# Two shared allocations for the small tiles of a two-layer decoder kernel

## The chip, the cores and the metric

One core of a Trainium2 chip runs the whole program. The metric is device time in microseconds (us) of one execution: the median over the runs of one kernel. Times inside an execution come from one profiled execution of the kernel before.

## The reference

Two layers of a decoder with a model width of 1024 over 256 tokens, all in float32. Layer 0 attends by blocks (at 256 tokens there is one block, so this is causal attention), layer 1 takes the weighted difference of two softmax maps. A SwiGLU FFN of width 2816 follows each. Shift, scale and gate come from a conditioning vector.

```python
c_act = jax.nn.silu(c)
for i in range(DEPTH):
    mod = (c_act @ ada_w[i] + ada_b[i])[:, None, :]
    sh_a, sc_a, g_a, sh_f, sc_f, g_f = jnp.split(mod, 6, axis=-1)
    h = rms_norm(x, norm_g[i, 0]) * (1.0 + sc_a) + sh_a
    y = moba_attention(...) if i % 2 == 0 else diff_attention(...)
    x = x + g_a * rms_norm(y, norm_g[i, 1])
    h = rms_norm(x, norm_g[i, 2]) * (1.0 + sc_f) + sh_f
    x = x + g_f * rms_norm(swiglu(h, ffn_w_in[i], ffn_w_out[i]), norm_g[i, 3])
```

## The kernel before

**Split products.** Every large weight is loaded as float32 in pieces of 128 x 1024 elements into one of eight `raw` buffers (`wpair`, line 497 on). ScalarE writes its rounded high part (line 503), VectorE the rest (line 504), both into one of nine `ring` buffers of 8 KB per partition. A matmul of a weight is then three passes (`mm`, line 506 on): high by high, high by low, low by high. In `mm` (line 512) the stationary operand is a 128 x 128 block of the activation and the moving operand is 512 columns of the ring buffer:

```python
a = h[:, 1 if q == 2 else 0, k]
for p, (b, s) in zip(ps, W):
    nc.tensor.matmul(p[:, :n], a, b[:, 1 if q == 1 else 0, s], start=first and q == 0, stop=last and q == 2)
```

In `mmT` (line 526) it is the other way round: the stationary operand is a block of the ring buffer, and the moving operand is 256 columns of `hh`, the activation of both token tiles.

**Where activations lie.** `hh` holds the split activation that enters QKV, the output projection (`po`) and the first FFN product (`pg`, `pu`, and `pgu` for the last, narrow chunk). The FFN's middle activation `a` goes into four buffers that attention used for q and k: chunk number even into `qT0` (token tile 0) and `qT1` (token tile 1), odd into `kT0` and `kT1`. The second FFN product (`f2`, psum `pf`) has `a` as its stationary operand and a ring buffer `s_u` as its moving one.

**Stages of one execution.** The first conditioning products and the first QKV run to about 60 us, attention and output projection of layer 0 to about 150 us, its FFN to about 325 us, attention of layer 1 to about 450 us, its FFN to the end.

**Order.** Every operation is recorded first; `Schedule.run` then sets one order from a table of priorities and from modelled costs, and gives each buffer a slot of its class. After that the tiles are made in the order in which they are first used, one tag per slot:

```python
for o in order:
    for b in o.bufs:
        if b.cls in ("h0", "h1"):
            b.t = hh[:, int(b.cls[1])]
        elif b.cls and b.t is None:
            b.t = pools.get(b.cls, sb).tile(list(b.shape), b.dt, name=b.name, tag=f"{b.cls}_{b.slot}")
    o.fn()
```

**Small tiles.** `keep` makes tiles that live through the whole program; some are 128 x 1 to 128 x 8 elements (`ones1`, `mh`, `cact`, the `scsh` vectors and others). `sm` makes the vectors of one to four elements of the norms and softmaxes (`ss`, `ms`, `y`, `mx`, `su`, `r`, `so`), in 24 slots. Each small tile and each of the 24 slots is an allocation of its own, which takes a multiple of 32 bytes in every partition, and they are mixed with the large tiles in the order of first use. So a large tile begins 0 or 32 bytes after a multiple of 64.

Of the kernel before, what the change touches and what calls it, by code (L numbers as in the profile page):

```python
# [12 lines left out]
F = mybir.dt.float32  # L13
# [219 lines left out]
def trunk_kernel(ctx: ExitStack, tc: tile.TileContext, x, c, rel_bias, ada_w, ada_b, norm_g, moba_w_qkv, moba_w_o,  # L233
# [4 lines left out]
    const = ctx.enter_context(tc.tile_pool(name="const", bufs=1))  # L238
    sb = ctx.enter_context(tc.tile_pool(name="sb", bufs=1))
# [4 lines left out]
    slots = dict(a=4, bc=4, raw=8, ring=9, z=2, acc=2, s2=8, qT0=1, qT1=1, kT0=1, kT1=1, PT0=2, PT1=2,  # L244
                 v0=1, v1=1, h0=1, h1=1, gate=2, sm=24)
    S_ = Schedule(slots)
    op = S_.op

    def keep(name, shape, dt=F):
        return Buf(name, t=const.tile(list(shape), dt, name=name))  # L250

    def sm(name, w=1):
        return Buf(name, "sm", [128, w])
# [8 lines left out]


    xt = [keep(f"x{t}", [128, D]) for t in range(T)]
    ident = keep("ident", [128, 128])
    ones = keep("ones", [128, 128], R)
    ones1 = keep("ones1", [128, 1])
    mh = keep("mh", [128, 4])
# [616 lines left out]

    order = S_.best()
    pools = dict.fromkeys(("a", "bc"), psum)
    for o in order:
        for b in o.bufs:
            if b.cls in ("h0", "h1"):  # L890
                b.t = hh[:, int(b.cls[1])]
            elif b.cls and b.t is None:
                b.t = pools.get(b.cls, sb).tile(list(b.shape), b.dt, name=b.name, tag=f"{b.cls}_{b.slot}")
        o.fn()
# [102 lines left out]
```

## Time and profile before

| | |
|---|---|
| median of 3 runs | 645.5 us (643.41 to 646.35) |
| the profiled execution's own time | 644.03 us |
| its span, first to last instruction | 642.1 us |
| TensorE busy | 630.3 us (98% of the span) |
| VectorE busy | 474.2 us (74%) |
| ScalarE busy | 366.7 us (57%) |
| share of TensorE in the chain that ended last | 82% |

The span is the part of the profiled execution that the trace covers; some 1.9 us of its own time lie around it. "Busy" adds up the durations of an engine's instructions, where overlapping matmuls count once. The chain is followed back from the last instruction to what released each step; its pieces add up to the span, so a piece of it is time that counts. Granted clock is TensorE's: 1.00 is 2.4 GHz, 0.50 is 1.2 GHz.

### The profile page before, as it was taken

The numbers are of one execution on the slowest core, as the hardware profiler recorded it, in microseconds if no ns is written. First come the engines' busy times: TensorE is split into PE (matmuls) and PEld (weight loads), VectorE is DVE, ScalarE is ACT, GpSimd is POOL, SyncE is SP. The second block draws the span as 40 slices with busy tenths as digits, with TensorE's granted clock in tenths as the row PEclk, the third lists the DMA queues.
The fourth block names the chain that finished last, engine by engine and source line by source line (L and its number), as shares of the span: only waits on it lengthen the run. The fifth ranks groups of instructions, "written<-read, shape, count | busy, mean of one in ns | idle before, by whom it ended". The sixth has DMA issues, their size and how long they took to land.

```text
span 642.1 us, 8916 instructions
## 1 busy us (share of the span) xinstructions
PE 630.3 (98%) x3216; PEld 524.7 (82%) x3216; DVE 474.2 (74%) x603; ACT 366.7 (57%) x616; POOL 31.1 (5%) x66
## 2 busy tenths in 40 slices
PE   8999989999999999999999999999999999999996
PEld 7899978887888888888887997888888888888884
DVE  2798689987788797646599999999546566744453
ACT  4567779378463634444396787949744453543342
POOL 1000000040000000000021000111100000000001
PEclk9799999999999999999999999999999999999999
DMA  9999999998999987657858988455467868645301
GB/s 306 360 335 333 320 332 362 362 308 271 331 306 379 312 304 261 197 167 235 279 194 295 358 284 284 134 174 183 147 219 231 266 220 265 203 141 165 114 1 65
DMA packets 72503, 160.60 MB, mean 250 GB/s; under 512 B 5506, under 2 KB 22531, under 8 KB 72459
## 3 DMA queue, kind: packets, MB, share of 16 engines
q1 hardware_dynamic: 72267, 159.96, 74.2%
q8 instruction: 25, 0.41, 0.3%
q14 instruction: 19, 0.16, 0.1%
q10 hardware_dynamic: 192, 0.08, 0.0%
HBM read 158.69 MB, written 1.33 MB: 249 GB/s over the span
## 4 chain that ended last, share of the span: by engine, by line
PE 82%; DMA 5%; DVE 5%; ACT 3%; issue 2%; POOL 1%; DVEq 0%; POOLq 0%; SPq 0%; ACTq 0%
PE pf L512 18%; PE pu L512 17%; PE pg L512 17%; PE po L512 5%; PE pv L512 5%; DMA bias<-toep 4%; PE pq L526 4%; PE pgu L512 3%; PE pq L512 2%; PE warm L307 2%; PE po L696 2%; PE pa L299 1%; DVE a L379 1%; ACT s_q L503 1%; DVE s_q L504 1%
## 5 line engine op out<-in xcount | busy, mean ns | idle before, releaser
L512 PE MATMUL pg<-s_i,hh 128*128 128x512 f32 x480 | 190.6, 397 | 0.1
L512 PE MATMUL pu<-s_i,hh 128*128 128x512 f32 x480 | 189.6, 395 | 0.0
L504 DVE TENSOR_TENSOR s_i<-w_i,s_i 128x1024 fp32r<-128x1024 f32 (+1 forms) x96 | 107.5, 1133 | 60.3 <-ACT s_i L503 60.0
L503 ACT ACTIVATE s_i<-w_i 128x1024 fp32r<-128x1024 f32 (+1 forms) x96 | 94.1, 987 | 89.7 <-PE pu L512 45.1
L512 PE MATMUL pf<-s_u,a 128*128 128x512 f32 x528 | 140.5, 397 | 0.0
L512 PEld LDWEIGHTS pf<-s_u,a 128*128 128x128 f32 x528 | 97.8, 188 | 22.3 <-ACT a L841 0.4
L512 PEld LDWEIGHTS pg<-s_i,hh 128*128 128x128 f32 x480 | 90.1, 188 | 21.9 <-ACT hh L548 0.5
L512 PEld LDWEIGHTS pu<-s_i,hh 128*128 128x128 f32 x480 | 90.2, 188 | 21.2
L379 DVE SCALAR_TENSOR_TENSOR acc<-aw,cact,acc 128x1024 f32<-128x1024 f32 x70 | 89.1, 1278 | 3.1 <-DMA aw<-in_ada_w_dram 2.5
L503 ACT ACTIVATE s_u<-w_u 128x1024 fp32r<-128x1024 f32 x44 | 46.5, 1059 | 58.5 <-PE pu L512 36.7
L504 DVE TENSOR_TENSOR s_u<-w_u,s_u 128x1024 fp32r<-128x1024 f32 x44 | 53.5, 1223 | 30.9 <-ACT s_u L503 30.5
L526 PE MATMUL pq<-hh,s_q 128*128 128x256 f32 x480 | 61.5, 285 | 0.7 <-ACT hh L548 0.7
L526 PEld LDWEIGHTS pq<-hh,s_q 128*128 128x128 f32 x480 | 59.3, 190 | 2.8 <-issue 0.9
L512 PE MATMUL po<-s_o,hh 128*128 128x512 f32 x192 | 50.3, 403 | 0.0
L512 PEld LDWEIGHTS po<-s_o,hh 128*128 128x128 f32 x192 | 35.0, 188 | 7.2
L504 DVE TENSOR_TENSOR s_q<-w_q,s_q 128x1024 fp32r<-128x1024 f32 x32 | 38.3, 1219 | 2.2 <-ACT s_q L503 2.2
L503 ACT ACTIVATE s_q<-w_q 128x1024 fp32r<-128x1024 f32 x32 | 32.9, 1056 | 6.7 <-DMA w_q<-in_moba_w_qkv_dram 4.1
L491 POOL TENSOR_SCALAR ms<-ss 128x1 f32<-128x1 f32 x16 | 9.4, 588 | 510.3 <-ACT z L577 502.0
L512 PE MATMUL pgu<-s_i,hh 128*128 128x512 f32 x96 | 26.5, 398 | 0.0
L512 PE MATMUL pv<-s_q0v,hh 128*128 128x512 f32 x96 | 24.9, 401 | 0.9 <-ACT s_q0v L503 0.9
L658 ACT ACTIVATE sx<-sx,mx 128x256 f32<-128x256 f32 (+1 forms) x48 | 21.3, 445 | 6.9 <-DVE mx L656 6.8
L512 PE MATMUL pv<-s_q1v,hh 128*128 128x512 f32 x96 | 24.7, 403 | 0.0
(142 smaller groups left out, 724.9 us busy)
## 6 DMA issues: line engine op xcount, KB each, us to landing
aw<-in_ada_w_dram SPq DMA_DIRECT2D x80, 512.0 KB
w_i<-in_ffn_w_in_dram SPq DMA_DIRECT2D x80, 512.0 KB
w_u<-in_ffn_w_out_dram SPq DMA_DIRECT2D x44, 512.0 KB
aw<-in_ada_w_dram SPq DMA_DIRECT2D x32, 256.0 KB
w_q<-in_moba_w_qkv_dram SPq DMA_DIRECT2D x16, 512.0 KB
w_q<-in_diff_w_qkv_dram SPq DMA_DIRECT2D x16, 512.0 KB
w_q0v<-in_moba_w_qkv_dram SPq DMA_DIRECT2D x8, 512.0 KB
w_o<-in_moba_w_o_dram SPq DMA_DIRECT2D x8, 512.0 KB
```

The lines of the kernel that those rows point to most:

```text
L299: nc.tensor.transpose(dst[:, o:o + n], a, ident[:n, :n])
L307: nc.tensor.matmul(warm.t[:].rearrange("p (a b) -> p a b", a=4), ones.t[:], ones.t[:, None, :].to_broadcast([128, 4, 128]), start=True, st ...
L379: op("DVE", tt(n) + 0.065, lambda: nc.vector.scalar_tensor_tensor(a.t, w(), cact[:, kc:kc + 1], a.t, op0=OP.mult, op1=OP.add), r=[cact, w. ...
L491: op("POOL", 0.16, lambda: nc.gpsimd.tensor_scalar(ms.t, m0.t[:], 1.0 / n, EPS, op0=OP.mult, op1=OP.add), r=[m0], w=[ms])
L503: op("ACT", ac(2 * n), lambda: nc.scalar.activation(b[:, 0], w.t[:], AF.Copy), r=[w], w=[(b, K(0))], name="hi" + name)
L504: op("DVE", tt(2 * n), lambda: nc.vector.tensor_sub(b[:, 1], w.t[:], b[:, 0].bitcast(F)), r=[w, (b, K(0))], w=[(b, K(1))], name="lo" + name)
L512: nc.tensor.matmul(p[:, :n], a, b[:, 1 if q == 1 else 0, s], start=first and q == 0, stop=last and q == 2)
L526: nc.tensor.matmul(p[:, j * 256:j * 256 + 256].rearrange("p (t q) -> p t q", t=T), b[:, 1 if q == 1 else 0, s, c + j * 128:c + j * 128 + 1 ...
L658: op("ACT", ac(nk, 2), lambda i=i, sx=sx, mx=mx, su=su: nc.scalar.activation(sx[:, i], sx[:, i], AF.Exp, bias=mx[:, i:i + 1], accum_out=su ...
L696: nc.tensor.matmul(p[:, i * 128:i * 128 + 128], a, b, start=kt == 0, stop=kt == t)
```

## The change

Small tiles no longer have allocations of their own. One allocation `small` (128 x 112 elements) holds what `keep` used to make with at most eight elements in a row, at steps of 16 or 32 bytes; one allocation `smt` (128 x 192) holds the 24 slots of `sm`, at steps of 32 bytes.

```diff
+    small = const.tile([128, 112], F, name="small")
+    small_at = [0]
+
     def keep(name, shape, dt=F):
-        return Buf(name, t=const.tile(list(shape), dt, name=name))
+        if len(shape) > 2 or shape[1] > 8:
+            return Buf(name, t=const.tile(list(shape), dt, name=name))
+        o = small_at[0]
+        small_at[0] += 4 if shape[1] <= 4 else 8
+        assert small_at[0] <= 112
+        return Buf(name, t=small[:shape[0], o:o + shape[1]])
 ...
+    smt = sb.tile([128, 8 * slots["sm"]], F, name="smt")
     for o in order:
         for b in o.bufs:
             if b.cls in ("h0", "h1"):
                 b.t = hh[:, int(b.cls[1])]
+            elif b.cls == "sm":
+                b.t = smt[:, 8 * b.slot:8 * b.slot + b.shape[1]]
             elif b.cls and b.t is None:
```

Every engine executes the same operations on tiles of the same shapes, in the same order. On TensorE, VectorE, GpSimd and SyncE each instruction also waits for the same semaphore values. On ScalarE 13 of 546 instructions wait at another place: a wait for GpSimd on a reused small slot stands one or two instructions later, and five instructions that only wait are gone.

What differs is where tiles begin. All large tiles have sizes that are multiples of 128 bytes, so without small ones between them they all begin at the same offset from a multiple of 128. Read from the two built programs, in bytes within a partition:

| tile | begins before, modulo 128 | begins now, modulo 128 |
|---|---|---|
| `hh` | 0 | 64 |
| `qT0`, `kT1` (hold `a`) | 96 | 64 |
| `kT0` (holds `a`) | 32 | 64 |
| `qT1` (holds `a`) | 0 | 64 |
| `ring` buffers (`s_q`, `s_i`, `s_u`, `s_o`) | 96 (eight of nine), 32 (one) | 64 |
| `raw` buffers | 96 or 32 (seven of eight), 0 (one) | 64 |
| `ones`, `ident`, `x` | 0 | 64 |

So every large tile now begins at a multiple of 64.

## Rows read from the trace of the kernel before

**Rows 1.** The page: span, and busy time, share and instructions of TensorE.

```profile
span 642.1 us, 8916 instructions
PE 630.3 (98%) x3216; PEld 524.7 (82%) x3216; DVE 474.2 (74%) x603; ACT 366.7 (57%) x616; POOL 31.1 (5%) x66
```

**Rows 2.** Busy time by stage: window, its length, each engine, granted clock, DMA.

```profile
core 0: us, PE busy (x) PEld busy (x) DVE busy (x) ACT busy (x) POOL busy (x), PEclk, DMA share, GB/s
0.00:60.00 60.00, 57.19 (x383) 52.91 (x384) 43.15 (x81) 34.06 (x61) 2.82 (x16) 0.91 1.01 336
60.00:150.00 90.00, 87.76 (x502) 74.89 (x501) 78.42 (x95) 65.81 (x134) 9.40 (x12) 1.00 0.99 333
150.00:325.00 175.00, 175.00 (x778) 141.53 (x777) 125.96 (x134) 85.56 (x104) 0.93 (x3) 1.00 0.79 270
325.00:450.00 125.00, 124.39 (x734) 105.71 (x733) 121.25 (x185) 97.06 (x209) 14.36 (x26) 1.00 0.73 245
450.00:642.10 192.10, 185.99 (x826) 149.66 (x824) 105.38 (x112) 84.25 (x111) 3.60 (x9) 1.00 0.52 169
```

**Rows 3.** The chain by line, windows 60:150, 150:325, 325:450 and 449:643.

```profile
by line: DMA bias<-toep 30.7%; PE po L512 13.6%; PE pv L512 13.0%; PE po L696 5.9%; issue 5.8%; ACT z L577 3.1%; PE ppt L299 2.7%; DVE x L590 2.5%; POOL ms L493 2.1%; ACT hm L543 2.1%; DVE z L587 2.1%; POOL y L494 1.9%; DVE z L557 1.5%; DVE
...
by line: PE pf L512 30.9%; PE pu L512 29.6%; PE pg L512 29.4%; PE pgu L512 6.4%; PE pa L299 2.6%; PE pgr L482 0.3%; PE pgr L483 0.3%; ACT sg L837 0.2%; issue 0.2%; PE pgc L401 0.2%; ACT z L577 0.1%
...
by line: PE pq L526 18.5%; PE pv L512 18.3%; PE po L512 18.0%; PE pq L512 10.8%; ACT s_q L503 5.2%; PE ps L648 4.8%; PE po L696 4.3%; ACT z L577 2.3%; PE pg L512 2.2%; ACT hm L543 2.1%; PE ppt L299 2.1%; PE pu L512 2.1%; POOL ms L491 1.6%; 
...
by line: PE pf L512 31.6%; PE pg L512 27.8%; PE pu L512 27.8%; PE pgu L512 5.8%; PE pa L299 2.5%; PE ph L299 0.5%; DVE x L590 0.4%; DVEq L993 0.3%; ACT z L577 0.3%; POOLq L993 0.3%; PE pgr L482 0.2%; PE pgr L483 0.2%; issue 0.1%; POOL ms L4
```

**Rows 4.** Chain pieces (start us, us, what): stationary `hh`, first and last of eight, then 23.

```profile
515.85 0.23 PE pu L512
...
517.48 0.24 PE pg L512
...
116.68 5.37 PE po L512 x23
```

**Rows 5.** Chain pieces of `pf`: `a` in `qT0`, `kT1`, `kT0`, `qT1`; last, `qT0`.

```profile
623.26 2.04 PE pf L512 x9
...
530.21 1.81 PE pf L512 x8
...
318.10 2.80 PE pf L512 x12
...
629.25 3.26 PE pf L512 x14
...
192.89 0.93 PE pf L512 x4
```

**Rows 6.** Busy time, columns as in rows 2, around three of those pieces.

```profile
530.20:532.00 1.80, 1.80 (x10) 1.36 (x8) 0.37 (x1) 1.06 (x1) 0.00 (x0) 1.00 0.71 216
623.30:625.30 2.00, 2.00 (x10) 1.66 (x9) 0.00 (x0) 0.00 (x0) 0.00 (x0) 1.00 0.00 0
629.30:632.50 3.20, 3.20 (x15) 2.59 (x14) 2.77 (x5) 0.84 (x4) 0.93 (x3) 1.00 0.00 0
```

**Rows 7.** Chain pieces just before 623.26, and the 512-column warm-up matmuls.

```profile
622.33 0.23 PE pgu L512
622.56 0.70 PE pf L512 x3
...
7.98 0.93 PE warm L307 x4
```

**Rows 8.** Chain pieces of line 526 (256 columns), and the transposes of `a` by line.

```profile
372.19 4.89 PE pq L526 x40
...
L299 PE MATMUL pa<-ident,sg 128*128 128x128 f32 x88 | 13.5, 272 | 0.0
```

**Rows 9.** VectorE and ScalarE on `w_u`: count, then ns minimum/median/maximum.

```profile
L503 ACT ACTIVATE s_u<-w_u x44: 1041/1060/1104, 161.3 to 616.8; 128x1024 fp32r<-128x1024 f32 x44
L504 DVE TENSOR_TENSOR s_u<-w_u,s_u x44: 1215/1224/1227, 162.4 to 617.9; 128x1024 fp32r<-128x1024 f32 x44
```

## The prediction

> **What bounds the kernel now.** I read the page first: TensorE is busy 630.3 of 642.1 us [rows 1]. A busy engine can still be one that waits in small pieces, so the busy times by stage come next [rows 2]. In the two FFN stages (150 to 325 us, and 450 us to the end) TensorE is busy all the time but for the last few us, the clock is at its upper level (1.00, 2.4 GHz), and DMA, VectorE and ScalarE have room. In the first 150 us the DMA share is about 1, and from 325 to 450 us VectorE is busy for 121.25 of 125 us. The chain of waits says the same [rows 3]: in the FFNs the matmuls of 512 columns (`pf`, `pu`, `pg`, `pgu`) are 96.3% and 93.0% of the chain, that is 168.5 us of 175 and 179 us of 193. So the time hangs on how fast matmuls of 512 columns follow each other, and the question is whether the place of a tile in memory changes that pace.
>
> The duration of a matmul in the trace doesn't tell the pace, since matmuls overlap; the length of a chain piece divided by its count does. I looked for pieces whose tiles I can name, and set them beside the table of offsets in the section on the change. Where the stationary operand is `hh` (offset 0) and the moving one a ring buffer (offset 96, modulo 128), eight pieces begin 1.63 us from first to last, seven steps of 233 ns; a run of 23 in the output projection takes 5.37 us, 233.5 ns each [rows 4]. In the second FFN product the stationary operand changes its buffer [rows 5]. With `a` in `qT0` (96) and a ring buffer at 96, nine take 2.04 us: 226.7 ns each. With `a` in `kT1` (also 96) eight take 1.81 us: 226.3 ns. With `a` in `kT0` (32) against 96, twelve take 2.80 us: 233.3 ns. With `a` in `qT1` (0) against 96, fourteen take 3.26 us: 232.9 ns. The last row is the one ring buffer at 32 with `a` in `qT0` at 96: four take 0.93 us, 232.5 ns. The reading is: **equal offsets modulo 128 give 226.7 ns, unequal ones 233.3 ns**, 6.6 ns or 2.8% more. Other traffic doesn't explain it [rows 6]: the piece at 226.3 ns (530 us) stands beside a DMA share of 0.71 and a busy ScalarE, the one at 232.9 ns (629 us) beside no DMA at all.
>
> The short step doesn't begin at once. The four pieces ahead of the nine at 226.7 ns take 0.93 us, 232.5 ns each, the first of them with `hh`, three already at equal offsets [rows 7]. So after a break of the pattern some four or five matmuls still go at about 232 ns.
>
> **The change part by part.** *Small tiles into two allocations:* the same operations with the same shapes; ScalarE loses five instructions that only wait, and 13 of its waits stand a little later. ScalarE is busy about half of each FFN stage [rows 2], so I cost this at nothing; it would count only if ScalarE became late for TensorE.
>
> *Large tiles move, for VectorE and ScalarE:* the 44 splits of `w_u` read all eight `raw` buffers and write the ring buffers, at all the mixed offsets of today, and VectorE's durations lie between 1215 and 1227 ns, ScalarE's between 1041 and 1104 [rows 9]. With medians of 1224 and 1060 this bounds a common offset to under 2% in either direction, on engines that aren't the bound in the FFNs: nothing.
>
> *Large tiles move, for the transfers:* no row tells one buffer's transfers from another's. The chain of 60 to 150 us holds 27.6 us of transfers (30.7% of 90) [rows 3]; half a per cent either way would be 0.1 us, and I take nothing. The Trainium skill (DMA: Bandwidth & Descriptors, "How a descriptor splits into AXI transactions") speaks against the change here: a piece that doesn't start at a multiple of 256 bytes costs one transaction more. One `raw` buffer of eight starts at such a multiple before and none does now, so by that page one load in eight of 2 KB pieces would need nine transactions in place of eight; as an estimate that is some 1.5% of the 90 us with a DMA share of 0.99, or plus 1.4 us. No row here shows it.
>
> *Large tiles move, for TensorE:* every pair of operands is now at equal offsets (64 and 64). The sum, piece by piece:
> - FFNs, 347.5 us of chain in 512-column matmuls. `pf` is 30.9% of 175 and 31.6% of 193, together 115 us; half of its matmuls have equal offsets already (`qT0` and `kT1` against the eight ring buffers). So 290 us go at unequal offsets, and 2.8% of that is 8.2 us. The other 57 us mix 226.7 and 232 ns and may gain 0 to 1 us as their neighbours stop breaking the pattern; I take 0.5.
> - Breaks remain: 88 transposes of `a` [rows 8] in groups of two to four, so some 22 to 44 breaks of five matmuls at 232 instead of 226.7 ns, 27 ns each: 0.6 to 1.2 us to give back. I take 0.9.
> - 325 to 450 us: `po`, `pv`, `pq` of line 512, `pg` and `pu` are 51.4% of the chain, 64 us; 2.8% is 1.8 us. VectorE has only 3.75 us of room in this stage [rows 2], so I count half, 0.9.
> - 60 to 150 us: `po` and `pv` are 26.6% of 90 us; 2.8% is 0.7 us, beside a DMA share of 0.99. I count 0.2.
> - Line 526 (ring buffer stationary, `hh` moving, 256 columns) takes 122 ns in a run of 40 [rows 8], always at unequal offsets. What equal offsets give there no row shows: between nothing and the same 6.6 ns each, which on 23 us of chain (18.5% of 125) is up to 1.3 us. I take nothing, since its stage is the one short of VectorE.
>
> 8.2 + 0.5 - 0.9 + 0.9 + 0.2 = 8.9 us. Against the profiled execution's 644.03 us this is 635.1; that execution is 0.2% under the median of the runs, 645.5, from which the same sum gives 636.6. I put the forecast between them, at **635.8 us**. With every uncertain term at its best (8.2 + 1.0 - 0.6 + 1.8 + 0.7 + 1.3) the gain is 12.4 us, from 644.03 a time of 631.6. If the next limit came up, it would be VectorE between 325 and 450 us; in the FFNs it has over 49 us of room.
>
> **The rivals.** *The offset is not the cause.* The short steps could come from something else that the two places share, for instance that no matmul there waits. For it: the warm-up matmuls have `ones` as both operands, so equal offsets, and four of them take 0.93 us, 232.5 ns [rows 7]; they stand so soon after a break that they may not have settled, and they read 128 columns four times over. Against it: seven places [rows 4, 5], busy and quiet, sort by offset alone. Then the time stays at 644 to 645.5 us. The Trainium skill (TensorE: Matmul & The Clock Gate, Part 2, "Step-by-step") stands on this side: "Loading the next tile's weights doesn't steal SBUF read bandwidth from the running matmul", so by it the two operands' places shouldn't matter to each other. The rows of 226.7 and 233.3 ns differ in just that.
>
> *The gain is partial.* The pattern is broken too often to settle, so that matmuls stay near 231.5 ns. Then 290 us gain 0.8%, 2.3 us, with the rest some 3 us: 641 us. The run of nine at 623 us settled within five, which speaks against it.
>
> *Slower.* All tiles at one offset could bring the weight load and the stream into each other's way for good. The place would be every 512-column matmul, 1490 of them on the FFN chain (347.5 us at 233 ns). From 235.5 ns on, 2.2 ns more each, that is 3.3 us and counts; at 237 ns it would be 649 us. For it: 64 against 64 occurs nowhere in this trace, and only pairs at 96 show the short step. Against it: no run at equal offsets is above 233 ns.
>
> *The change doesn't do what it says.* The offsets in the built program are all 64, so only the rivals above remain.
>
> **How the numbers follow.** The forecast (632 to 639 us) gets 0.66, the partial gain 0.12, no effect 0.13, slower 0.09. Half a per cent, 3.2 us, is about what a measurement of this kernel can tell from no change. The partial gain lies at that bound and is halved: faster 0.66 + 0.06 = 0.72, same 0.06 + 0.13 = 0.19, slower 0.09. The range goes from 631, where all uncertain terms are at their best, to 643, which takes in the partial gain and leaves out most of no effect and all of slower, about 0.2 together.
>
> **What would show it.** In the new trace, runs of `pg` and `pu` in the FFNs should step by about 227 ns, with four or five at 232 after each group of transposes; the two FFN stages should be 8 us shorter together. `pf` from `qT1` and `kT0` should be as fast as from `qT0`. VectorE's 1224 ns and ScalarE's 1060 ns should stand. The prediction is wrong in its mechanism if `pg` and `pu` still step by 233 ns, and wrong in its sum if they step by 227 and the stage between 325 and 450 us, or the first 150 us, gets longer.

## The result, and the profile after

| kernel | median us (lowest to highest) | ratio to before, 95% interval |
|---|---|---|
| before | 644.45 (642.31 to 646.35) | |
| changed | 636.17 (634.17 to 636.36) | 0.9865 [0.9825, 0.9905] |
| changed, measured again beside the kernel before | 635.19 (633.97 to 636.89) | 0.9866 [0.9844, 0.9887] |

The changed kernel is 1.35% faster, 8.3 us between the medians; the forecast was 635.8 us. Its profiled execution has a span of 634.5 us, 7.6 us under the 642.1 of before. The page of the changed kernel, span and busy times, answers to [rows 1]:

```profile
span 634.5 us, 8911 instructions
PE 621.5 (98%) x3216; PEld 525.8 (83%) x3216; DVE 473.8 (75%) x603; ACT 367.1 (58%) x616; POOL 31.9 (5%) x66
```

TensorE's busy time fell by 8.8 us with the same 3216 instructions; VectorE, ScalarE and GpSimd stand within 0.8 us of before. Busy time by stage in the changed kernel, columns as in [rows 2]; the borders are set where its own stages end:

```profile
core 0: us, PE busy (x) PEld busy (x) DVE busy (x) ACT busy (x) POOL busy (x), PEclk, DMA share, GB/s
0.00:60.00 60.00, 57.21 (x379) 53.45 (x379) 42.78 (x81) 33.65 (x61) 2.83 (x16) 0.89 1.02 335
60.00:150.00 90.00, 87.12 (x505) 75.34 (x504) 78.41 (x94) 65.85 (x135) 9.42 (x12) 1.00 0.99 333
150.00:322.00 172.00, 172.00 (x780) 141.91 (x779) 126.37 (x135) 86.31 (x107) 0.93 (x3) 1.00 0.80 275
322.00:442.00 120.00, 119.04 (x716) 102.18 (x715) 116.75 (x180) 94.06 (x202) 14.07 (x24) 1.00 0.72 245
442.00:634.50 192.50, 186.16 (x844) 152.92 (x842) 109.48 (x117) 87.28 (x116) 4.61 (x11) 0.99 0.54 176
```

The stages look as in [rows 2]: TensorE fills the first FFN stage, and VectorE is busy for 97% of the second attention stage, as before. Fixed windows hide where time went, so I take landmarks: the first matmul of each product. The tile view gives count, ns minimum/median/maximum, then the first and last start in us. First the kernel before:

```profile
L512 PE MATMUL pv<-s_q0v,hh x96: 388/396/498, 75.1 to 109.7; 128*128 128x512 f32 x96
L512 PE MATMUL pg<-s_i,hh x240: 388/394/503, 139.5 to 301.2; 128*128 128x512 f32 x120
L512 PE MATMUL pq<-s_q,hh x96: 388/394/484, 332.5 to 362.3; 128*128 128x512 f32 x96
L512 PE MATMUL pg<-s_i,hh x240: 388/394/477, 442.5 to 612.9; 128*128 128x512 f32 x120
L512 PE MATMUL pf<-s_u,a x528: 387/394/482, 171.4 to 635.6; 128*128 128x512 f32 x176
```

and the changed kernel, in which line 512 has become 521:

```profile
L521 PE MATMUL pv<-s_q0v,hh x96: 387/389/500, 75.8 to 110.2; 128*128 128x512 f32 x96
L521 PE MATMUL pg<-s_i,hh x240: 387/389/499, 139.8 to 298.4; 128*128 128x512 f32 x120
L521 PE MATMUL pq<-s_q,hh x96: 387/389/477, 329.2 to 358.9; 128*128 128x512 f32 x96
L521 PE MATMUL pg<-s_i,hh x240: 387/389/486, 438.8 to 605.7; 128*128 128x512 f32 x120
L521 PE MATMUL pf<-s_u,a x528: 387/389/486, 171.2 to 628.0; 128*128 128x512 f32 x176
```

The start of one landmark taken from the start of the next gives a stage:

| stage | before, us | changed, us | difference | predicted |
|---|---|---|---|---|
| start to first `pv` | 75.1 | 75.8 | +0.7 | 0 |
| first `pv` to first `pg` (attention, layer 0) | 64.4 | 64.0 | -0.4 | -0.2 |
| first `pg` to first `pq` (FFN, layer 0, and what leads to `pq`) | 193.0 | 189.4 | -3.6 | |
| first `pq` to next `pg` (attention, layer 1) | 110.0 | 109.6 | -0.4 | -0.9 |
| that `pg` to last `pf` (FFN, layer 1) | 193.1 | 189.2 | -3.9 | |
| the two FFN stages | 386.1 | 378.6 | -7.5 | -7.8 |
| last `pf` to end of span | 6.5 | 6.5 | 0 | 0 |

The median duration of one of these matmuls went from 394 to 389 ns. As they overlap, the pace (the step from one start to the next) is read from the chain of waits: the length of a piece divided by its count. Pieces of the changed kernel's chain (start us, us, what), in the order of [rows 4], [rows 5] and [rows 8]:

```profile
504.84 0.23 PE pu L521
...
506.43 0.23 PE pg L521
...
115.56 7.27 PE po L521 x32
...
615.20 3.64 PE pf L521 x16
...
621.11 7.30 PE pf L521 x32
...
368.80 4.98 PE pq L535 x40
```

From 504.84 to 506.43 there are seven steps, so 227 ns each, against 233 in [rows 4]; 32 steps of `po` in 7.27 us make 227.2 against 233.5 before. `pf` with `a` in `qT0` (615.20) takes 227.5 ns and with `a` in `qT1` (621.11) 228.1, both with some slower steps at their start that follow transposes; `qT1` stood at 232.9 in [rows 5].

### The profile page after: what moved, and what is told of

The parts are those of the page before. It is cut to its first block, busy times and chain, and to the rows that moved or that the text cites. A ratio compares the mean times of both kernels' runs of the same rounds, so it can differ in the third digit from the quotient of the medians.

```text
span 634.5 us, 8911 instructions
## 1 busy us (share of the span) xinstructions
PE 621.5 (98%) x3216; PEld 525.8 (83%) x3216; DVE 473.8 (75%) x603; ACT 367.1 (58%) x616; POOL 31.9 (5%) x66
## 3 DMA queue, kind: packets, MB, share of 16 engines
q1 hardware_dynamic: 72267, 159.96, 74.8%
## 4 chain that ended last, share of the span: by engine, by line
PE 81%; ACT 5%; DMA 4%; DVE 4%; issue 2%; POOL 2%; POOLq 0%; DVEq 0%; SPq 0%; ACTq 0%
PE pf L521 18%; PE pg L521 16%; PE pu L521 16%; PE po L521 5%; PE pv L521 5%; PE pq L535 5%; DMA bias<-toep 4%; PE pgu L521 3%; PE pq L521 2%; PE warm L316 2%; PE po L705 2%; ACT s_q L512 2%; PE pa L308 1%; ACT z L586 1%; ACT hm L552 1%
## 5 line engine op out<-in xcount | busy, mean ns | idle before, releaser
L521 PE MATMUL pg<-s_i,hh 128*128 128x512 f32 x480 | 188.2, 392 | 0.1
L521 PE MATMUL pu<-s_i,hh 128*128 128x512 f32 x480 | 187.0, 390 | 0.0
L521 PE MATMUL pf<-s_u,a 128*128 128x512 f32 x528 | 138.5, 393 | 0.0
L388 DVE SCALAR_TENSOR_TENSOR acc<-aw,small,acc 128x1024 f32<-128x1024 f32 x70 | 89.1, 1277 | 3.6 <-DMA aw<-in_ada_w_dram 2.9
L512 ACT ACTIVATE s_u<-w_u 128x1024 fp32r<-128x1024 f32 x44 | 46.6, 1060 | 57.0 <-PE pu L521 30.9
L535 PE MATMUL pq<-hh,s_q 128*128 128x256 f32 x480 | 62.6, 288 | 0.7 <-ACT hh L557 0.7
L500 POOL TENSOR_SCALAR smt<-smt 128x1 f32<-128x1 f32 (+1 forms) x20 | 10.5, 526 | 581.6 <-ACT z L586 495.2
L667 ACT ACTIVATE sx<-sx,smt 128x256 f32<-128x256 f32 (+1 forms) x48 | 21.3, 446 | 6.3 <-DVE smt L665 6.1
```

The costliest lines, as they stand in the source:

```text
L388: op("DVE", tt(n) + 0.065, lambda: nc.vector.scalar_tensor_tensor(a.t, w(), cact[:, kc:kc + 1], a.t, op0=OP.mult, op1=OP.add), r=[cact, w. ...
L500: op("POOL", 0.16, lambda: nc.gpsimd.tensor_scalar(ms.t, m0.t[:], 1.0 / n, EPS, op0=OP.mult, op1=OP.add), r=[m0], w=[ms])
L512: op("ACT", ac(2 * n), lambda: nc.scalar.activation(b[:, 0], w.t[:], AF.Copy), r=[w], w=[(b, K(0))], name="hi" + name)
L535: nc.tensor.matmul(p[:, j * 256:j * 256 + 256].rearrange("p (t q) -> p t q", t=T), b[:, 1 if q == 1 else 0, s, c + j * 128:c + j * 128 + 1 ...
L667: op("ACT", ac(nk, 2), lambda i=i, sx=sx, mx=mx, su=su: nc.scalar.activation(sx[:, i], sx[:, i], AF.Exp, bias=mx[:, i:i + 1], accum_out=su ...
```

## The experiments

Two theories go into them; both would explain the result, since the change made all offsets equal and also made them all multiples of 64. **Match:** the step depends on whether the stationary and the moving operand begin at the same offset (the prediction said: modulo 128). **Alignment:** what counts is that tiles begin at a multiple of 64, wherever the other operand is. All edits below start from the changed kernel. "Offset" is a byte address within a partition.

### All tiles at one offset that is no multiple of 64

```diff
-    small = const.tile([128, 112], F, name="small")
+    small = const.tile([128, 104], F, name="small")
 ...
```

> The changed kernel with the shared allocation `small` 32 bytes shorter: every large tile begins at 32 modulo 128, so operands still match each other, but nothing begins at a multiple of 64. If matching offsets are the cause, nothing is lost against the changed kernel: 636 us, `pg` and `pu` step by 227 ns. If the multiple of 64 is the cause, the gain is gone: 644 us, 233 ns a step.

Measured: 635.82 us, ratio 0.9863 [0.9824, 0.9901]. Two pieces of its chain:

```profile
340.98 6.85 PE pq L521 x30
...
620.75 7.30 PE pf L521 x32
```

228.3 and 228.1 ns per step with every large tile at 32 modulo 128: as good as the changed kernel. Both pieces include a few slow steps after a break. A multiple of 64 is not needed.

### All at multiples of 64, but `hh` 64 bytes away from the rest

```diff
-    smt = sb.tile([128, 8 * slots["sm"]], F, name="smt")
+    smt = sb.tile([128, 4 * slots["sm"] + 16], F, name="smt")
-                b.t = smt[:, 8 * b.slot:8 * b.slot + b.shape[1]]
+                b.t = smt[:, 4 * b.slot:4 * b.slot + b.shape[1]]
```

> The changed kernel with 64 bytes of padding behind `hh` (the slots of `sm` at steps of 16 bytes make room): every large tile still begins at a multiple of 64, but `hh` lies 64 bytes apart from all ring buffers modulo 128; `a` and the ring buffers match. If matching offsets are the cause, `pg`, `pu`, `pgu`, `po`, `pv` and `pq` step by 233 ns and `pf` by 227: only the half of `pf` that did not match before is won, 57 us by 2.8% = 1.6 us, so about 643 us. If the multiple of 64 is the cause: 636 us and 227 ns everywhere.

Measured: 642.17 us, 0.9972 [0.9954, 0.9991]. Its chain:

```profile
114.04 7.47 PE po L521 x32
...
343.22 7.00 PE pq L521 x30
...
626.73 7.33 PE pf L521 x32
```

Every tile begins at a multiple of 64, as in the changed kernel, and yet `po` and `pq`, which read `hh` as stationary operand, take 233.4 and 233.3 ns. Only `pf`, whose `a` still matches the ring buffers, keeps 229.1. 6.4 of the 8.7 us that the kernel with all at 32 gained beside it are gone. **Match holds, and alignment alone doesn't give the gain.**

### `small` alone

The kernel with the shared `small`, and the slots of `sm` each with an allocation of its own, as before. `hh`, `qT0`, `kT1` and eight ring buffers then stand at 64 modulo 128; `qT1` (96), `kT0` (0) and one ring buffer (0) don't.

```diff
-    smt = sb.tile([128, 8 * slots["sm"]], F, name="smt")
 ...
-            elif b.cls == "sm":
-                b.t = smt[:, 8 * b.slot:8 * b.slot + b.shape[1]]
```

> The allocation `small` alone, the 24 slots of `sm` as before. `hh` and eight of nine ring buffers then match (64), one ring buffer lies at 0; `a` matches in `qT0` and `kT1` and not in `qT1` (96) and `kT0` (0), as before. If matching offsets are the cause, the `hh` matmuls win eight ninths of their part, 232 us by 2.8% = 5.8 us in the FFNs, less 0.9 for breaks, and some 1 us in attention, and `pf` nothing: 638.5 us. If the multiple of 64 is the cause, all but `qT1` is won: 637 us, with `pf` from `kT0` at 227 ns instead of 233. The steps of `pf` from `kT0` tell the two apart, not the time.

Measured: 637.56 us, 0.9906 [0.9873, 0.994]. Its chain, `pf` with `a` in `qT0` and then in `qT1`:

```profile
616.35 3.64 PE pf L520 x16
...
622.29 7.46 PE pf L520 x32
```

227.5 ns where the operands match, 233.1 where they don't, a few us apart in one execution. So the gain comes in parts, pair by pair; most of it came with `hh`.

The pair that was to tell the theories apart, `pf` with `a` in `kT0`, fits neither:

```profile
314.86 2.76 PE pf L520 x12
```

These twelve take 230.0 ns each, with single steps between 226 and 236, where match expected 233 and alignment 227. `kT0` and the ring buffers are 192 bytes apart modulo 256 here, as in the kernel before, where the same piece took 233.3 ns [rows 5]; both tiles begin 32 bytes lower. So the distance alone doesn't set the pace of every unequal pair.

### The modulus: 128 bytes apart

`hh` 128 bytes away from the ring buffers: equal modulo 128, unequal modulo 256. The edit is that of `hh` 64 bytes away, without the padding:

```diff
+    smt = sb.tile([128, 4 * slots["sm"] + 0], F, name="smt")
+                b.t = smt[:, 4 * b.slot:4 * b.slot + b.shape[1]]
```

> The changed kernel with `hh` 128 bytes apart from all ring buffers modulo 256 (64 against 192; the slots of `sm` at steps of 16 bytes); every large tile at a multiple of 64, all equal modulo 128; `a` and the ring buffers match fully. By my rule of the prediction (a match modulo 128 is enough): 636 us, 227 ns a step with `hh`. By what the first scan showed for 128 bytes (229 to 241 ns, uneven): `pg`, `pu`, `po`, `pv`, `pq` at 232 to 233 ns and 642 us, as with 64 bytes apart.

Measured: 642.44 us, 0.9981 [0.9967, 0.9995]. Its chain, and its row of `pg` in the tile view:

```profile
115.03 7.44 PE po L521 x32
...
344.17 7.00 PE pq L521 x30
```

```profile
L521 PE MATMUL pg<-s_i,hh x240: 390/393/477, 442.1 to 611.7; 128*128 128x512 f32 x120
```

232.5 and 233.3 ns, and `pg` at 393 ns: about as slow as 64 bytes apart. **Equal modulo 128 is not enough; equal modulo 256 is.** Equal modulo 512 isn't needed: by the built programs `hh` and the ring buffers of the changed kernel are 256 bytes apart modulo 512, `a` and the ring buffers 0, and both settle at 227 ns. The pairs of the kernel before that were equal modulo 128 were also equal modulo 256, so its trace couldn't tell the two apart.

### Other distances

Two kernels, executed once each, move the buffers of `a` against the ring buffers by padding and shift; `hh` matches (both with `small` of 104 elements and `smt` at steps of 16 bytes):

```diff
+    SHIFT = {'qT0': 0, 'kT0': 4, 'kT1': 1}       # second kernel: 12, 2, 28
+            elif b.cls in SHIFT and b.t is None:
+                n, e = math.prod(b.shape[1:]), SHIFT[b.cls]
+                t = sb.tile([b.shape[0], n + 32], b.dt, name=b.name, tag=f"{b.cls}_{b.slot}")[:, e:e + n]
 ...
```

The distances, modulo 256, are 128 (`qT0`), 16 (`kT0`), 132 (`kT1`), 0 (`qT1`) in the first, and 176, 8, 240, 0 in the second. (The two texts below give some of them modulo 128.)

> A scan in one execution: the changed kernel's layout (slots of `sm` at steps of 16 bytes), with the four buffers of `a` shifted against the ring buffers: `qT0` by 128 bytes, `kT0` by 16, `kT1` by 4, `qT1` by 0. `hh` matches. Read from the runs of `pf` by buffer. If offsets must match modulo 128: `qT0` and `qT1` step by 227 ns once settled. If a match modulo 256 is needed: `qT0` by 233. For 16 and 4 bytes: 227 if what must match is a block of 32 bytes or more, 233 if it is the exact place. The whole kernel then takes 636 to 638 us.

> The same scan with `qT0` shifted by 48 bytes, `kT0` by 8, `kT1` by 112, `qT1` by 0. By a match within 32-byte blocks: `kT0` 227 ns, `qT0` and `kT1` 233. By a match of the exact place: only `qT1` at 227, the three others at 233, and 638 to 639 us.

Measured: 636.27 and 637.04 us, one execution each. Chain pieces of the first, `a` in `qT0`, then in `qT1`:

```profile
614.99 3.70 PE pf L521 x16
...
620.96 7.30 PE pf L521 x32
```

128 bytes apart takes 231 ns, 0 apart 228.1: the result of `hh` 128 bytes away, seen with another operand. From the starts of the matmuls one by one in the two traces, the settled steps are 226.7 ns at 132 bytes; at 16 bytes some stretches of 226.7 and some of 233; at 240 bytes 226.7 or 229; at 176 bytes 226 to 236 in turn and at 8 bytes 229 to 234, 230 to 231 in the mean. Neither rule that the two texts name, a block of 32 bytes or the exact place, gives this pattern. So "unequal gives 233.3" holds for long stretches at 64 and 160 bytes, nearly at 128 (232.4 in the mean with `hh`), and not for every distance: 192 bytes gave 233.3 in one kernel and 230.0 in another, and 224 bytes occur in stretches of at most six matmuls.

To see whether 16 bytes give both steps with `hh` too, `hh` was shifted by 16 bytes (`smt` as in the case of 128 bytes):

```diff
-    hh = const.tile([128, T, 2, KC, 128], R, name="hh")
+    hh = const.tile([128, T * 2 * KC * 128 + 32], R, name="hh")[:, 4:4 + T * 2 * KC * 128].rearrange(
+        "p (t s k c) -> p t s k c", t=T, s=2, k=KC)
```

> The same with `hh` 16 bytes apart from all ring buffers; `a` and the ring buffers match. By an exact match as the condition: 642 us and 233 ns with `hh`. By the scan, where 16 bytes showed both 226.7 and 233 ns: some runs at 227 and some at 233, so between 636 and 642 us. By a match within a block of 32 bytes: 636 us.

Measured: 635.9 us, 0.9891 [0.9876, 0.9907]. Its chain:

```profile
113.27 7.47 PE po L521 x32
...
340.56 6.82 PE pq L521 x30
```

One long stretch at 233.4 ns and another at 227.3, each with `hh` and a ring buffer at the same distance. `po` itself steps by 233.4 ns at 113 us and, by its starts, by 226.7 at 413 us. At 16 bytes the pace is one of two, and which one it is must hang on something other than the distance: not settled here. In the FFNs it was mostly the short one: by the landmarks they took 380.3 us, against 378.6 matched and 384.6 with 128 bytes, so the time is near that of a match.

### All large tiles at multiples of 256

The small tiles in two allocations of 32 and 96 elements, `smt` with 4 elements for each of its 24 slots and 32 of padding; matched as in the changed kernel, but at 0 modulo 256. It asks about the transfers, for which the prediction had named a rule against the change.

```diff
-    small = const.tile([128, 112], F, name="small")
+    smalls = [const.tile([128, 32], F, name="small")]
 ...
+    smalls.append(const.tile([128, 96], F, name="small2"))
+    small_at[0] = 0
 ...
+    smt = sb.tile([128, 4 * slots["sm"] + 32], F, name="smt")
 ...
```

> All large tiles at multiples of 256 (the small ones in two allocations placed so, the slots of `sm` at steps of 16 bytes). If matching offsets are the cause for TensorE and the transfers don't care: 636 us as the changed kernel, and the weight queue's share of the DMA engines stays at 74 to 75%. By the Trainium skill (DMA: Bandwidth & Descriptors, How a descriptor splits into AXI transactions) pieces that begin at a multiple of 256 need one transaction less, eight instead of nine for 2 KB: then that share falls to about 68 to 70% and the first 150 us, where the DMA share is near 1, get several us shorter: 630 to 633 us.

> The changed kernel once more, on the same chip as the next one: 636 us, 0.985 to 0.99 of the kernel before.

> All large tiles at multiples of 256 once more, beside the changed kernel. If only matching offsets count: the same time within 0.5% (3 us), any difference lying in the first 60 us, where the granted clock falls at another moment in each execution. If the start at a multiple of 256 helps the transfers: 2 to 3 us less than the changed kernel again, all of it in the first 150 us, with a lower share of the weight queue.

Measured: 633.6 us, 0.9843 [0.9813, 0.9874], and in the second comparison 633.72, 0.9845 [0.9824, 0.9867], with the changed kernel beside it at 635.19. The queue of the loads on the page (packets, MB, time of the packets as a share of 16 engines' span), at 256, then in the changed kernel:

```profile
q1 hardware_dynamic: 72267, 159.96, 74.9%
```

```profile
q1 hardware_dynamic: 72267, 159.96, 74.8%
```

The time lies between the two that were expected, and the share hardly moves (in the second comparison 74.2% against 75.2%). Some of the single transfers do get shorter. Counted packet by packet in the traces, those of 512 bytes took 27.1 and 27.4 ns in the mean in the two profiles with all at 256, against 29.3 to 30.1 in the ten profiles of the other kernels; those of 1024 bytes, the size of the rows of `bias`, 50.9 and 50.0 against 53.2 to 54.6. Those of 2048 and 4096 bytes didn't differ clearly. The chain from 60 to 150 us holds no transfer in either profile with all at 256; here it is in the first of them:

```profile
by line: PE pv L523 21.2%; PE po L523 13.3%; PE pk L537 12.8%; PE po L707 5.9%; PE ps L659 5.8%; issue 5.5%; PE ppt L310 3.2%; ACT z L588 3.1%; PE pg L523 2.8%; DVE z L598 2.8%; PE pu L523 2.6%; DVE x L601 2.5%; POOL smt L504 2.1%; ACT hm L
```

In each of the other ten profiles transfers are at least 19% of that stretch; in the kernel before they are 30.7% [rows 3], in the changed one 31.2%.

The time is 1.5 us under the changed kernel beside it in the second comparison, and in the first 2.2 us under the kernel with all tiles at 32 modulo 128; the intervals of the ratios overlap, but the sign is the same twice. By the tile view the difference lies around the first `pv` and `pg`:

```profile
L523 PE MATMUL pv<-s_q0v,hh x96: 387/389/504, 74.4 to 107.0; 128*128 128x512 f32 x96
L523 PE MATMUL pg<-s_i,hh x480: 387/389/496, 136.6 to 602.2; 128*128 128x512 f32 x160
```

From `pv` to `pg` it takes 62.2 us, and 61.4 in its second profile, against 64.0 and 63.5 in the changed kernel. The kernels with `hh` 64 and 16 bytes apart, with no tile at a multiple of 256, took 62.6 and 62.8 there by the same rows, so part of this comes without the 256. The shorter small packets and the chain without transfers speak for an effect of the 256 on loads. An estimate is a microsecond or so, from 62.2 and 61.4 us against 62.6 to 64.4 in all other kernels; no kernel moved the loads' tiles alone, so it is not shown.

## Why the prediction was right

**The mechanism** was read right from chain pieces of the same kind of matmul on different tiles: the step of 512-column matmuls hangs on whether the two operands' offsets match. Matching at another offset kept the gain, and unmatching `hh` alone took 6.4 us of it away. The rival that the offset is not the cause falls with that. On its side stood a sentence of the Trainium skill (TensorE: Matmul & The Clock Gate, Part 2, "Step-by-step"): loading the next weights steals no read bandwidth from the running matmul. What the prediction drew from it, that the two operands' places shouldn't matter to each other, doesn't agree with 7.47 us for 32 steps of `po` with `hh` 64 bytes apart against 7.27 us matched. The runs show that the two operands' places matter to each other; by what path in the chip, they don't show.

**The modulus** was wrong. The prediction wrote 128; a distance of 128 bytes is about as slow as one of 64. That this cost nothing was luck of the layout: `hh`, the buffers of `a` and the ring buffers all begin at 192 modulo 256 in the changed kernel. (`ones`, `ident` and `x` begin at 64; a few short products read `ones` against a large tile, 128 bytes apart.) With tiles of odd multiples of 128 bytes between them the rule as predicted would have failed. Also "unequal ones 233.3" was read from 160 and 192 bytes in stretches of some length; the reading for the one ring buffer at 32 had only four matmuls, no more than what the prediction itself counts as settling. Other distances behave otherwise, and 192 did so too in one kernel.

**The sum**, 8.9 us predicted, 7.6 in the span and 8.3 in the medians, step by step:
- FFNs: 7.8 predicted (8.2 + 0.5 - 0.9), 7.5 measured. The term for the breaks was of the right kind and somewhat short: by the starts of neighbouring matmuls, what the steps have over 226.7 ns adds up to 1.2 us in the two FFN stages of the changed kernel, where 0.9 was taken. After the transposes ahead of `kT0` (chain piece at 314 us) the trace has ten steps between 224 and 240 ns, 232 in the mean, and then 226 to 227; I had counted five to a break. `pf` from `kT0` is so as fast as from `qT0` once it has settled. Over all 1915 pairs of neighbouring 512-column matmuls of line 521 that start less than 260 ns apart the mean step is 227.7 ns; before it was 232.9, over 1918 pairs.
- Attention of layer 1: 0.9 predicted, 0.4 measured. VectorE's share of 97% there is what it was. A second cause is visible in line 526, now 535: 40 matmuls of 256 columns took 4.89 us [rows 8] and now take 4.98, at equal offsets. I had bounded equal offsets there between nothing and a gain; they cost. Both lengths hold one step of 222 or 223 ns at their start; the other 38 steps are 117.4 ns in the mean before and 119.7 now. Over all neighbours in that line (more than 450 in each kernel) it is 118.5 before and 119.6 to 119.7 in every kernel with `hh` matched to all ring buffers. How much of the missing 0.5 us goes to which of the two was not separated.
- Attention of layer 0: 0.2 predicted, 0.4 measured.
- Up to the first `pv`: 0 predicted, 0.7 us longer. The granted clock over the first 60 us is 0.89 against 0.91 [rows 2]. The kernel with all tiles at multiples of 256 had its first `pv` at 74.4 us in one profile and at 76.1 in the other, so this wanders by more than 0.7 us between executions of one kernel, and I don't hold it to be the change's.
- VectorE and ScalarE, taken at nothing: the splits of `w_u` in the changed kernel have the medians of [rows 9], 1061 for 1060 and 1225 for 1224:

```profile
L512 ACT ACTIVATE s_u<-w_u x44: 1042/1061/1102, 161.4 to 609.5; 128x1024 fp32r<-128x1024 f32 x44
L513 DVE TENSOR_TENSOR s_u<-w_u,s_u x44: 1214/1225/1226, 162.5 to 610.6; 128x1024 fp32r<-128x1024 f32 x44
```

**The other rivals.** The partial gain fell because the stretches between breaks are long enough: the last stretch of `pf` has 32 steps, of which seven are slow. Slower fell since 64 against 64 takes what 96 against 96 took, 226 to 227 ns. The estimate of 1.4 us against the change stood on a rule of the Trainium skill (DMA: Bandwidth & Descriptors, "How a descriptor splits into AXI transactions"). The page tells of the bytes that a transaction reads; that it holds for writes into `raw` was the prediction's own step. No such cost is seen: packets of 2048 bytes took 97.8 ns in the mean before and after, and the queue's share was 74.2% and 74.8%. With all tiles at 256 the small packets did get shorter, as told above; that this is the rule's doing is not shown.

## What to carry to other kernels

Where matmuls follow each other without gaps, look up at what offset modulo 256 the stationary and the moving tile begin, and make them equal. One odd small allocation ahead of the large ones shifts all that follow, so keep small tiles in a shared one of a round size. Read the pace from long chain pieces, length by count, and name the tiles of each piece: the mean over a kernel hides two paces 2.8% apart, and over the `pf` of the kernel before it hides them almost wholly (231.8 ns for equal pairs and 232.2 for unequal ones in the FFN stages), since few of its stretches were long enough to settle. A modulus that is read from one layout is only as good as the distances that occur in it, so try one distance between the candidates before it becomes a rule.

## What the runs showed of the hardware that was not expected

- The step of matmuls of 512 columns in fp32r settles at 226.7 ns at equal offsets modulo 256. It is 233.3 ns 64 bytes apart and 232.4 ns 128 bytes apart with `hh`, all at a granted clock of 1.00.
- At 16 bytes both paces occur with `hh` and a ring buffer (7.47 us for 32 and 6.82 us for 30).
- At 256 columns (line 535) equal offsets cost a little: 119.7 ns a step in the mean, 118.5 before.
- After transposes of `a` one to twelve steps, most often nine or ten, go at about 232 ns in the changed kernel before the short one sets in.
- With all large tiles at multiples of 256 bytes, packets of 512 and 1024 bytes took 4 to 10% less in both profiles.
